# Rotary embedding on one core: the first load grows from 512 rows to 1024, and one table layout serves all tiles

## The chip, the core and the metric

The kernel runs on one core of a Trainium2 chip. The metric is device time in microseconds (us), the median over runs. Five engines work side by side: TensorE (PE), VectorE (DVE), ScalarE (ACT), GpSimd (POOL) and SyncE (SP). Each executes its own instructions in order and waits on semaphores for the others. Transfers (DMAs) are issued from the instruction streams of ACT and SP here, and 16 DMA engines, which both queues share, carry them out.

## The reference

`x` is 16 batches x 512 sequence positions x 1024 values in float32 (33.6 MB); `cos` and `sin` have 512 rows of 32 values. Each row of 1024 values is 16 heads of 64, and each head is rotated:

```python
x = x.reshape(batch, seq, num_heads, head_dim)
x1, x2 = x[..., :half_dim], x[..., half_dim:]
cos = cos[None, :, None, :]; sin = sin[None, :, None, :]
rotated = concatenate([x1 * cos - x2 * sin, x1 * sin + x2 * cos], axis=-1)
```

So for every row: t1 = x times cos, t2 = (x with the halves of each head swapped) times (-sin, +sin), and the result is t1 + t2. The table row depends on the sequence position alone.

## The kernel before

**Units.** The work is cut into 64 units `u` (the code's `rows`): a unit is 128 partitions x 1024 values, so 128 rows of `x`. Eight units, 0 to 7, 8 to 15 and so on, are called a group here: 1024 rows of `x`, 4 MB. A group is 8 slots of the ring `x_sb`, which holds 5 groups; results are written over the inputs in the ring and stored from there.

**Tiles.** A tile is what one DMA loads and one DMA stores. Batches 0, 1, 14 and 15 are `singles`: 512 rows, 4 per partition, 2 MB. The twelve batches between are taken in pairs, 8 rows per partition, 4 MB. So the first and the last group consist of two tiles of four units each, and the other six groups of one tile each. In a pair tile, partition `2 s + b` holds rows `8 s` to `8 s + 7` of batch `b` of the pair.

**Tables.** A single needs cos and sin with four sequence positions per partition (partition `p`: 4p to 4p+3); a pair needs eight (partitions 2s and 2s+1: 8s to 8s+7). The tables are loaded once into `stage` in the layout of singles. For singles, DVE copies cos to PSUM (L273) and ACT writes (-sin, +sin) to `s1_sb` (L183, L184). For pairs, two TensorE matmuls with a 0/1 matrix `pick`, made from the identity matrix, gather the rows into `pair_ps` (L209); ACT then writes `s2_sb` (L187, L188), and DVE makes a small PSUM table for its own sine products just before the first pair (L280, L281).

**A unit.** DVE multiplies x by cos into one of three PSUM buffers (`mul`, L302). POOL multiplies the swapped x by the sine table into one of eight SBUF buffers `t2_sb` (L263), two units in one instruction where `G2` says so. In row 3 of each pair tile DVE does that product instead of POOL (`V2`, L295). The sum is made by DVE (`comb`, L313), or, for units 1, 3 and 5 of a group (`PE2`; in the first and last group only some of them), by TensorE, which adds t2 onto t1 in PSUM (L225), and ACT, which copies the sum back to the ring (L192).

**Order.** All orders are written out by hand. DVE runs `mul(u)` one unit ahead of `comb`. The loads of the first five groups are issued by ACT at the start: the first tile, the two tables, then the rest. The later loads stand in ACT's stream behind the copy of a unit: the load of group 5 behind unit 17, of group 6 behind unit 25, and the two of group 7 behind unit 33. Each first waits until the stores of the ring slots that it overwrites have landed (`sem_out[k]`, line 195; groups 0, 1 and 2). While ACT waits there, the copies behind it wait too, and DVE stops when it needs the PSUM buffer of a unit that ACT has not copied. SP issues the stores, each when its tile's last sums are done (line 160).

Of the kernel before, what the change touches and what calls it, by code (L numbers as in the profile page):

```python
# [6 lines left out]
def bass_split_heads_rope_kernel(  # L7
# [16 lines left out]
    batch, seq, dim = x.shape  # L24
# [12 lines left out]
    COPY = mybir.ActivationFunctionType.Copy  # L37


    singles = (0, 1, batch - 2, batch - 1)  # L40
    tiles = [(b, R1 if b in singles else R2) for b in range(batch) if b in singles or b % 2 == 0]
    NT = len(tiles)
    RING = 5 * R2

    rows = [(t, r) for t, (_, n) in enumerate(tiles) for r in range(n)]
    NU = len(rows)
    EARLY = (NU - RING) // R2


    V_ROW = 3  # L50
    PE2 = [R1 <= u < NU - R1 and u % R2 in (1, 3, 5) for u in range(NU)]
    V2 = [tiles[t][1] == R2 and r == V_ROW for t, r in rows]

    def count(flags):
        return [sum(flags[: u + 1]) for u in range(NU)]
# [16 lines left out]
    with ExitStack() as stack:  # L72
        x_sb = stack.enter_context(nc.sbuf_tensor([P, RING, H, 2, HALF], fp32))
        t2_sb = stack.enter_context(nc.sbuf_tensor([P, NT2, H, 2, HALF], fp32))
        stage = stack.enter_context(nc.sbuf_tensor([P, 2, R1 * HALF], fp32))
        s1_sb = stack.enter_context(nc.sbuf_tensor([P, R1, 2, HALF], fp32))
        s2_sb = stack.enter_context(nc.sbuf_tensor([P, R2, 2, HALF], fp32))
        ident = stack.enter_context(nc.sbuf_tensor([P, P], fp32))
        pick = stack.enter_context(nc.sbuf_tensor([P, 2, P // 2, 2], fp32))
        zero = stack.enter_context(nc.sbuf_tensor([P, BANK], bf16))  # L80
        tab_ps = stack.enter_context(nc.psum_tensor([P, BANK], fp32))
        pair_ps = stack.enter_context(nc.psum_tensor([P, 2, 2, R1, HALF], fp32))
        t1_ps = stack.enter_context(nc.psum_tensor([P, NT1, H * HD], fp32))
        sem_in = [stack.enter_context(nc.semaphore(f"in{t}")) for t in range(NT)]
        sem_out = [stack.enter_context(nc.semaphore(f"out{k}")) for k in range(EARLY)]
# [13 lines left out]
        sem_t = stack.enter_context(nc.semaphore("pairs"))  # L99
        sem_a = stack.enter_context(nc.semaphore("act"))  # L100

        c1_ps = tab_ps[:, 0:R1 * HALF].rearrange("p (r d) -> p r d", d=HALF)
        v_ps = tab_ps[:, R1 * HALF:R1 * HALF + HD].rearrange("p (t d) -> p t d", d=HALF)

        def c_of(t, r):
            return c1_ps[:, r, :] if tiles[t][1] == R1 else pair_ps[:, r // R1, 0, r % R1, :]

        x1 = x.rearrange("b (s r) d -> b s (r d)", r=R1)
        o1 = out.rearrange("b (s r) h d -> b s (r h d)", r=R1)
        x2 = x.rearrange("b (s r) d -> s b (r d)", r=R2)  # L110
        o2 = out.rearrange("b (s r) h d -> s b (r h d)", r=R2)
        xs = x_sb[:].rearrange("p n h t d -> p n (h t d)")

        def in_dram(single, pairs, t):
            b, n = tiles[t]
            return single[b] if n == R1 else pairs[:, b:b + 2, :]

        def in_sbuf(t):
            b, n = tiles[t]
            k = b * R1 % RING  # L120
            return x_sb[:, k:k + n].rearrange("p n h t d -> p (n h t d)")

        def where(u):
# [3 lines left out]
        def swapped(k):  # L127
            return x_sb[:, k, :, ::-1, :]

        def over_heads(table):  # L130
            return table[:, None, :, :].broadcast_to([P, H, 2, HALF])
# [16 lines left out]

        def stores_of(k):

            return sum(b * R1 // R2 == k for b, _ in tiles)

        def load(eng, t):
            eng.dma_start(in_sbuf(t), in_dram(x1, x2, t)).then_inc(sem_in[t], 16)  # L154

        def on_sync(sp):
            for u in range(NU):
                t, r, k = where(u)
                if r == tiles[t][1] - 1:
                    wait_added(sp, u)  # L160
                    k = u // R2
                    sp.dma_start(in_dram(o1, o2, t), in_sbuf(t)).then_inc(sem_out[k] if k < EARLY else sem_rest, 16)
            sp.wait_ge(sem_rest, 16 * sum(stores_of(k) for k in range(EARLY, NU // R2)))

        def on_scalar(ae):
            later = {}
            for t, (b, n) in enumerate(tiles):
                if b * R1 + n <= RING:
                    load(ae, t)
                else:  # L170

                    later.setdefault((b * R1 - RING) // R2 * R2 + R2 - 1 + LAG, []).append(t)
                if t == 0:
                    for i, (table, sem) in enumerate(((cos, sem_cos), (sin, sem_sin))):
                        ae.dma_start(stage[:, i, :], table.rearrange("(s r) d -> s (r d)", r=R1)).then_inc(sem, 16)  # L175

            ae.wait_ge(sem_i, 2)
            ae.activation(  # L178
                pick[:], ident[:].rearrange("q (s k) -> q k s", k=2)[:, :, :, None].broadcast_to([P, 2, P // 2, 2]), COPY
            ).then_inc(sem_g, 1)  # L180
            ae.wait_ge(sem_sin, 16)
            sv = stage[:, 1, :].rearrange("s (r d) -> s r d", d=HALF)
            ae.activation(s1_sb[:, :, 0, :], sv, COPY, scale=-1.0)  # L183
            ae.activation(s1_sb[:, :, 1, :], sv, COPY).then_inc(sem_s, 1)  # L184
            ae.wait_ge(sem_t, 2)
            s2 = s2_sb[:].rearrange("p (k r) t d -> p k r t d", r=R1)
            ae.activation(s2[:, :, :, 0, :], pair_ps[:, :, 1, :, :], COPY, scale=-1.0)  # L187
            ae.activation(s2[:, :, :, 1, :], pair_ps[:, :, 1, :, :], COPY).then_inc(sem_s, 1)  # L188
            for u in range(NU):
                if PE2[u]:  # L190
                    ae.wait_ge(sem_e, n_pe[u])
                    ae.activation(xs[:, u % RING, :], t1_ps[:, u % NT1, :], COPY).then_inc(sem_a, 1)  # L192
                for t in later.get(u, ()):
                    k = (tiles[t][0] * R1 - RING) // R2
                    ae.wait_ge(sem_out[k], 16 * stores_of(k))
                    load(ae, t)

        def on_tensor(pe):
# [4 lines left out]
                        t1_ps[:, k, b * BANK:(b + 1) * BANK], zero[:, 0:P], zero[:], start=True, stop=True  # L203
                    ).then_inc(sem_w, 1)
            pe.wait_ge(sem_g, 1)
            pe.wait_ge(sem_cos, 16)
            pe.wait_ge(sem_sin, 16)
            for k in range(2):
                pe.matmul(  # L209
                    pair_ps[:, k].rearrange("p c r d -> p (c r d)"),  # L210
                    pick[:, k].rearrange("q s b -> q (s b)"),
                    stage[:].rearrange("q c f -> q (c f)"),
                    start=True,
                    stop=True,
                ).then_inc(sem_t, 1)
# [19 lines left out]
        def on_gpsimd(pl):  # L235
# [11 lines left out]
            for u in range(NU):  # L247
                if V2[u] or (G2[u] and u % 2 == 1):
                    continue
                t, r, k = where(u)  # L250
                n = 2 if G2[u] else 1
                if (t, r) == (0, 0):
                    pl.wait_ge(sem_s, 1)
                if (t, r) == (2, 0):
                    pl.wait_ge(sem_s, 2)
                if r == 0:
                    pl.wait_ge(sem_in[t], 16)
                if n == 2 and u + 1 >= NT2:
                    pl.wait_ge(sem_m, u + 2 - NT2 + NT1)  # L259
                elif n == 1:  # L260
                    wait_t2_free(pl, u)
                table = (s1_sb if tiles[t][1] == R1 else s2_sb)[:, r:r + n]
                pl.tensor_tensor(  # L263
                    t2_sb[:, u % NT2:u % NT2 + n],
                    x_sb[:, k:k + n, :, ::-1, :],
                    table[:, :, None, :, :].broadcast_to([P, n, H, 2, HALF]),
                    mult,
                ).then_inc(sem_p, 1)

        def on_vector(ve):  # L270
            ve.memset(zero[:], 0.0).then_inc(sem_z, 1)  # L271
            ve.wait_ge(sem_cos, 16)
            ve.tensor_copy(c1_ps, stage[:, 0, :].rearrange("s (r d) -> s r d", d=HALF)).then_inc(sem_c, 1)  # L273
            ve.wait_ge(sem_c, 1)
            ve.wait_ge(sem_w, NT1 * EH)

            def pair_tables():
                ve.wait_ge(sem_s, 2)
                row = pair_ps[:, V_ROW // R1, 1, V_ROW % R1, :]
                ve.tensor_scalar_mul(v_ps[:, 0, :], row, -1.0).then_inc(sem_c, 1)  # L280
                ve.tensor_copy(v_ps[:, 1, :], row).then_inc(sem_c, 1)  # L281

            first_v = V2.index(True)

            def mul(u):
                t, r, k = where(u)
                if r == 0:
                    ve.wait_ge(sem_in[t], 16)
                if (t, r) == (2, 0):
                    pair_tables()  # L290
                if u == first_v:
                    ve.wait_ge(sem_c, 3)
                if V2[u]:
                    wait_t2_free(ve, u)
                    ve.tensor_tensor(t2_sb[:, u % NT2, :, :, :], swapped(k), over_heads(v_ps), mult)  # L295
                if u >= NT1:
                    v = u - NT1
                    if PE2[v]:
# [3 lines left out]
                ve.tensor_tensor(  # L302
                    t1_ps[:, u % NT1, :].rearrange("p (h d) -> p h d", d=HALF),
                    x_sb[:, k, :, :, :].rearrange("p h t d -> p (h t) d"),
                    c_of(t, r)[:, None, :].broadcast_to([P, 2 * H, HALF]),
                    mult,
                ).then_inc(sem_m, 1)

# [55 lines left out]
```

## Time and profile before

| what | value |
|---|---|
| time, median of 3 runs (lowest, highest) | 161.18 us (161.13, 161.49) |
| span of the profiled execution, first to last instruction | 159.6 us |
| median time less that span | 1.6 us |
| DMA moved, mean rate over the span | 67.25 MB, 421 GB/s |
| POOL busy, DVE busy | 131.7 us (82%), 129.6 us (81%) |
| PE busy, ACT busy | 64.4 us (40%), 24.3 us (15%) |

The execution that was profiled has no time of its own beside its span. The span runs from the first to the last instruction, and the last is SP's wait for the last store, so the span holds all transfers. Busy shares are averages over stages; which engine ends a stage has to be read from the stage.

### The profile page before, as it was taken

What the parts mean: (1) busy time and instruction counts of PE and PEld (TensorE: products, weight loads), DVE (VectorE), ACT (ScalarE), POOL (GpSimd) and SP (SyncE); (2) the same over time, 40 slices, a digit from 0 to 9 for tenths busy, and PEclk for the clock granted to TensorE, in tenths of its full rate; (3) what the DMA queues carried; (4) which work ended last, traced back from release to release, by engine and by line L of the source; (5) the groups of instructions that cost most, each with busy time, mean ns of one, the idle gap of its engine ahead of it and who ended that gap; (6) DMA issues with size and microseconds to landing.
All of it is one profiled execution on the core that took longest, in us unless ns stands there. A gap on an engine that the chain in (4) does not pass through costs nothing.

```text
span 159.6 us, 499 instructions
## 1 busy us (share of the span) xinstructions
PE 64.4 (40%) x94; PEld 22.2 (14%) x94; DVE 129.6 (81%) x117; ACT 24.3 (15%) x27; POOL 131.7 (82%) x41
## 2 busy tenths in 40 slices
PE   6050017076408870789067400575058506900000
PEld 1020011021102220222021100211021102300000
DVE  0069947999999989998999629999999999556900
ACT  0420002004300250023102040023202310220000
POOL 1069999999999999999999798992999999089400
PEclk9999999759985589557759985589957995585555
DMA  5999999999999999999999999999999999999997
GB/s 144 396 466 472 394 411 431 448 476 402 394 448 406 495 419 402 476 435 402 443 435 435 394 476 435 402 460 394 427 456 448 443 394 423 472 419 435 386 456 300
DMA packets 3169, 67.25 MB, mean 421 GB/s; under 512 B 352, under 2 KB 608, under 8 KB 608
## 3 DMA queue, kind: packets, MB, share of 16 engines
q10 hardware_dynamic: 1728, 33.69, 49.8%
q1 hardware_dynamic: 1440, 33.56, 48.9%
q14 instruction: 1, 0.01, 0.0%
HBM read 33.69 MB, written 33.55 MB: 421 GB/s over the span
## 4 chain that ended last, share of the span: by engine, by line
DMA 61%; DVE 17%; POOL 5%; PE 5%; issue 4%; ACTq 1%; ACT 1%; DVEq 0%; POOLq 0%; SPq 0%
DMA x_sb<-in_x_dram 43%; DMA out_dram<-x_sb 18%; DVE t_ps L302 8%; DVE x_sb L313 7%; POOL t_sb L263 5%; PE t_ps L225 5%; DVE t_sb L295 2%; ACT x_sb L192 1%; ACTq L154 1%; ACTq L175 1%; DVE tab_ps L280 0%; DVEq L312 0%; DVE tab_ps L281 0%; DVEq L299 0%; POOLq L259 0%
## 5 line engine op out<-in xcount | busy, mean ns | idle before, releaser
L263 POOL TENSOR_TENSOR t_sb<-x_sb,s_sb 128x2048 f32<-128x2048 f32 (+1 forms) x35 | 131.0, 3784 | 17.1 <-DMA x_sb<-in_x_dram 8.3
L225 PE MATMUL t_ps<-t_sb,ident 128*128 128x512 f32 x84 | 59.6, 857 | 69.1 <-DVE t_ps L302 56.7
L302 DVE TENSOR_TENSOR t_ps<-x_sb,pair_ps 128x1024 f32<-128x1024 f32 x48 | 57.5, 1221 | 5.2 <-ACT x_sb L192 5.2
L313 DVE TENSOR_TENSOR x_sb<-t_ps,t_sb 128x1024 f32<-128x1024 f32 x43 | 52.2, 1216 | 5.9 <-POOL t_sb L263 5.9
L192 ACT ACTIVATE x_sb<-t_ps 128x1024 f32<-128x1024 f32 x21 | 21.4, 1024 | 107.6 <-PE t_ps L225 99.9
L225 PEld LDWEIGHTS t_ps<-t_sb,ident 128*128 128x128 f32 x84 | 20.3, 267 | 108.2 <-DVE t_ps L302 78.7
L302 DVE TENSOR_TENSOR t_ps<-x_sb,tab_ps 128x1024 f32<-128x1024 f32 x16 | 19.2, 1222 | 2.6 <-DMA x_sb<-in_x_dram 2.5
L295 DVE TENSOR_TENSOR t_sb<-x_sb,tab_ps 128x1024 f32<-128x1024 f32 x6 | 7.3, 1209 | 0.0
L273 DVE COPY tab_ps<-stage 128x128 f32<-128x128 f32 x1 | 0.3, 296 | 7.6 <-DMA stage<-in_cos_dram 7.6
L209 PE MATMUL pair_ps<-stage,pick 128*128 128x256 f32 x4 | 2.0, 667 | 5.1 <-DMA stage<-in_sin_dram 5.1
L202 PE MATMUL t_ps<-zero 128*128 128x512 bf16 x6 | 2.7, 629 | 1.3 <-DVE zero L271 1.3
L178 ACT ACT_TABLE_LOAD x1 | 1.3, 1283 | 5.5 <-issue 5.5
L209 PEld LDWEIGHTS pair_ps<-stage,pick 128*128 128x128 f32 x4 | 1.2, 324 | 6.1 <-issue 6.0
L202 PEld LDWEIGHTS t_ps<-zero 128*128 128x128 bf16 x6 | 0.7, 136 | 2.4 <-DVE zero L271 1.2
L271 DVE MEMSET zero<- 128x256 uint32 x1 | 0.3, 272 | 0.9 <-PEq L346 0.9
L187 ACT ACTIVATE s_sb<-pair_ps 128x256 f32<-128x256 f32 x1 | 0.4, 384 | 1.7 <-PE pair_ps L209 1.7
L183 ACT ACTIVATE s_sb<-stage 128x128 f32<-128x128 f32 x1 | 0.3, 310 | 1.8 <-DMA stage<-in_sin_dram 1.8
L236 POOL MEMSET ident<- 128x128 f32 x1 | 0.2, 205 | 0.3 <-POOLq L346 0.3
L178 ACT ACTIVATE pick<-ident 128x256 f32<-128x256 f32 x1 | 0.4, 416 | 0.0
L188 ACT ACTIVATE s_sb<-pair_ps 128x256 f32<-128x256 f32 x1 | 0.4, 377 | 0.0
L238 POOL TENSOR_SCALAR_AFFINE_SELECT ident<-ident 128x128 f32<-128x128 f32 x1 | 0.3, 295 | 0.1
L346 POOL MEMSET const-float32-0.0<- 128x1 f32 x1 | 0.1, 99 | 0.3 <-issue 0.3
(6 smaller groups left out, 1.0 us busy)
## 6 DMA issues: line engine op xcount, KB each, us to landing
x_sb<-in_x_dram ACTq DMA_DIRECT2D x6, 4096.0 KB, 38.7
out_dram<-x_sb SPq DMA_DIRECT2D x6, 4096.0 KB, 25.3
x_sb<-in_x_dram ACTq DMA_DIRECT2D x4, 2048.0 KB, 22.7
out_dram<-x_sb SPq DMA_DIRECT2D x4, 2048.0 KB, 16.1
stage<-in_cos_dram ACTq DMA_DIRECT2D x1, 64.0 KB, 7.5
stage<-in_sin_dram ACTq DMA_DIRECT2D x1, 64.0 KB, 7.2
```

Of the source, the lines that this page charges most:

```text
L154: eng.dma_start(in_sbuf(t), in_dram(x1, x2, t)).then_inc(sem_in[t], 16)
L175: ae.dma_start(stage[:, i, :], table.rearrange("(s r) d -> s (r d)", r=R1)).then_inc(sem, 16)
L178: ae.activation(pick[:], ident[:].rearrange("q (s k) -> q k s", k=2)[:, :, :, None].broadcast_to([P, 2, P // 2, 2]), COPY).then_inc(sem_g, 1)
L187: ae.activation(s2[:, :, :, 0, :], pair_ps[:, :, 1, :, :], COPY, scale=-1.0)
L192: ae.activation(xs[:, u % RING, :], t1_ps[:, u % NT1, :], COPY).then_inc(sem_a, 1)
L202: pe.matmul(t1_ps[:, k, b * BANK:(b + 1) * BANK], zero[:, 0:P], zero[:], start=True, stop=True).then_inc(sem_w, 1)
L209: pe.matmul(pair_ps[:, k].rearrange("p c r d -> p (c r d)"), pick[:, k].rearrange("q s b -> q (s b)"), stage[:].rearrange("q c f -> q (c f)"),
L225: ins = pe.matmul(t1_ps[:, u % NT1, b * BANK:(b + 1) * BANK], ident[:], t2[:, b * BANK:(b + 1) * BANK], start=False, stop=True, skip_group ...
L263: pl.tensor_tensor(t2_sb[:, u % NT2:u % NT2 + n], x_sb[:, k:k + n, :, ::-1, :], table[:, :, None, :, :].broadcast_to([P, n, H, 2, HALF]), ...
L295: ve.tensor_tensor(t2_sb[:, u % NT2, :, :, :], swapped(k), over_heads(v_ps), mult)
L302: ve.tensor_tensor(t1_ps[:, u % NT1, :].rearrange("p (h d) -> p h d", d=HALF), x_sb[:, k, :, :, :].rearrange("p h t d -> p (h t) d"), c_of ...
L313: ve.tensor_tensor(xs[:, k, :], t1_ps[:, u % NT1, :], t2_sb[:, u % NT2, :, :, :].rearrange("p h t d -> p (h t d)"), add,).then_inc(sem_v, 1)
```

## The change

All groups but the last become one tile of 1024 rows, the first group too. The rows of a tile are now numbered straight through: partition `64 b + s` holds rows `8 s` to `8 s + 7` of batch `b` of the pair, so a tile is 4 MB in one piece in DRAM, and no longer two batches interleaved partition by partition. The last group has the same layout but is loaded and stored in two halves, rows 0 to 3 and rows 4 to 7 of each partition (2 MB each, 16 KB pieces).

With one layout for all tiles there is one set of tables. `cos` and `sin` are loaded into 64 partitions, eight positions each. One matmul for each table, with `pick` now the 64 x 64 identity twice side by side, spreads it over 128 partitions, cos to `cos_bank` and sin to `sin_bank`. ACT makes one table `s_sb` from `sin_bank`. DVE's copy of cos (L273) and ACT's two copies for singles (L183, L184) are gone. DVE reads cos from `cos_bank` for all units; for its own sine products it uses two rows of `sin_bank` next to each other, the lower of which it overwrites with the negated row 3 (`v_table`, one small instruction, in the first group).

Since the first group is one tile, its unit 3 is now among the `V2` units: DVE makes that product, and POOL has one unit fewer (57 instead of 58). The issue points of the loads in ACT's stream, the sizes of the ring and of the buffers, and the split of the sums between DVE and TensorE stay.

```diff
-    singles = (0, 1, batch - 2, batch - 1)
-    tiles = [(b, R1 if b in singles else R2) for b in range(batch) if b in singles or b % 2 == 0]
+    runs = batch // 2
+    tiles = []
+    for c in range(runs):
+        if c == runs - 1:
+            tiles += [(c, 0, R1), (c, R1, R1)]
+        else:
+            tiles.append((c, 0, R2))
...
-        x2 = x.rearrange("b (s r) d -> s b (r d)", r=R2)
-        o2 = out.rearrange("b (s r) h d -> s b (r h d)", r=R2)
+        xr = x.rearrange("(c b) (s r) d -> c (b s) r d", b=2, r=R2)
+        outr = out.rearrange("(c b) (s r) h d -> c (b s) r (h d)", b=2, r=R2)
...
-                        ae.dma_start(stage[:, i, :], table.rearrange("(s r) d -> s (r d)", r=R1)).then_inc(sem, 16)
+                        ae.dma_start(stage[:, i, :], table.rearrange("(s r) d -> s (r d)", r=R2)).then_inc(sem, 16)
...
-            ae.wait_ge(sem_sin, 16)
-            sv = stage[:, 1, :].rearrange("s (r d) -> s r d", d=HALF)
-            ae.activation(s1_sb[:, :, 0, :], sv, COPY, scale=-1.0)
-            ae.activation(s1_sb[:, :, 1, :], sv, COPY).then_inc(sem_s, 1)
             ae.wait_ge(sem_t, 2)
-            s2 = s2_sb[:].rearrange("p (k r) t d -> p k r t d", r=R1)
-            ae.activation(s2[:, :, :, 0, :], pair_ps[:, :, 1, :, :], COPY, scale=-1.0)
-            ae.activation(s2[:, :, :, 1, :], pair_ps[:, :, 1, :, :], COPY).then_inc(sem_s, 1)
+            ae.activation(s_sb[:, :, 0, :], sin_ps, COPY, scale=-1.0)
+            ae.activation(s_sb[:, :, 1, :], sin_ps, COPY).then_inc(sem_s, 1)
...
-            pe.wait_ge(sem_cos, 16)
-            pe.wait_ge(sem_sin, 16)
-            for k in range(2):
+            for i, (table_ps, sem) in enumerate(((cos_ps, sem_cos), (sin_ps, sem_sin))):
+                pe.wait_ge(sem, 16)
                 pe.matmul(
...
-            ve.wait_ge(sem_cos, 16)
-            ve.tensor_copy(c1_ps, stage[:, 0, :].rearrange("s (r d) -> s r d", d=HALF)).then_inc(sem_c, 1)
-            ve.wait_ge(sem_c, 1)
             ve.wait_ge(sem_w, NT1 * EH)
+            ve.wait_ge(sem_t, 1)
+
+            def v_table():
+                ve.wait_ge(sem_s, 1)
+                ve.tensor_scalar_mul(sin_ps[:, V_ROW - 1, :], sin_ps[:, V_ROW, :], -1.0).then_inc(sem_c, 1)
...
-                if (t, r) == (2, 0):
-                    pair_tables()
+                if u == first_v - 1:
+                    v_table()
```

## The prediction

> **What bounds the kernel now.** I read the stretches of the span first, then the DMA queues, then the waits, then the timeline at the places where compute stops.
>
> Busy time by stretch (start:end, length, busy us of each engine with counts, granted PE clock, DMA share, GB/s):
> ```profile
> 0.00:1.80 1.80, 0.55 (x2) 0.28 (x3) 0.27 (x1) 0.00 (x0) 0.70 (x6) 1.00 0.00 0
> 1.80:3.40 1.60, 1.60 (x6) 0.46 (x4) 0.00 (x0) 0.00 (x0) 0.00 (x0) 1.00 1.15 225
> 3.40:20.00 16.60, 2.64 (x6) 1.18 (x4) 10.65 (x10) 2.87 (x6) 10.45 (x5) 1.00 1.01 428
> 60.00:100.00 40.00, 17.26 (x24) 5.91 (x24) 35.17 (x32) 6.04 (x6) 38.21 (x11) 0.72 1.00 433
> 100.00:140.00 40.00, 21.80 (x32) 7.43 (x32) 37.75 (x34) 7.34 (x8) 33.18 (x8) 0.77 1.01 433
> 140.00:158.40 18.40, 0.00 (x0) 0.00 (x0) 9.24 (x8) 0.86 (x1) 9.12 (x3) 0.56 0.98 421
> 158.40:159.60 1.20, 0.00 (x0) 0.00 (x0) 0.00 (x0) 0.00 (x0) 0.00 (x0) 0.50 0.23 96
> ```
> The last two figures say it: from 1.8 us to 158.4 us the 16 DMA engines are never idle, at 433 GB/s once started. No compute engine is full everywhere. Compute matters only if it leaves the DMA engines without a queued transfer, or issues the last store late.
>
> DMA engine time of a packet, from the DMA queue lines of two windows in which one size moves alone (packets, MB, share of 16 engines; 155 to 158 us, then 15 to 20 us):
> ```profile
> q1 hardware_dynamic: 78, 1.28, 99.3%
> q10 hardware_dynamic: 64, 2.10, 97.0%
> ```
> 78 packets of 16 KB in 99.3% of 16 x 3 us: 0.611 us each. 64 packets of 32 KB in 97.0% of 16 x 5 us: 1.2125 us each. So one 32 KB packet is 0.0095 us cheaper than two of 16 KB. A 4 MB tile of 128 packets of 32 KB is 8 per engine: 9.7 us alone, 19.4 us when the other queue takes every second packet.
>
> Waits:
> ```profile
> POOL t_sb L263 <- DMA x_sb<-in_x_dram: 8.3, 3, 4.3
> POOL t_sb L263 <- ACT s_sb L184: 8.2, 1, 8.2
> DVE t_ps L302 <- ACT x_sb L192: 5.2, 3, 4.4
> ```
> POOL waits for loads three times, so it has spare time in the middle. Its 8.2 us are the start. DVE's 4.4 us are seen in the timeline:
> ```profile
> 92.04 1.53 ACTq L154 DMA_DIRECT2D x_sb<-in_x_dram  x2
> 93.61 1.94 ACT L192 ACTIVATE x_sb<-t_ps 128x1024 f32<-128x1024 f32 x2 [7.78 <-issue]
> 94.67 2.36 DVE L302 TENSOR_TENSOR t_ps<-x_sb,pair_ps 128x1024 f32<-128x1024 f32 x2 [4.41 <-ACT x_sb L192]
> ```
> ACT stands before the loads of group 7 until group 2's store has landed (92.0), and DVE behind it. Last, the store that ends the run:
> ```profile
> 151.88 0.34 SPq L162 DMA_DIRECT2D out_dram<-x_sb  x1
> ```
> From the first load (issued 0.81, first packet at 1.8) a transfer needs 1.0 us to its first packet, so this one can move from 152.9. Packets end at 159.2 (0.4 us of landing before the span's end), and its 8 x 0.611 = 4.9 us begin at 154.3: even the last store waited 1.4 us for the DMA engines.
>
> **What the change does to the DMA sum.** Before: 1024 packets of 16 KB (four singles, in and out) and 1536 of 32 KB. After: 512 and 1792. That is 256 times 0.0095 us over 16 engines: -0.15 us. The tables go from 256 packets of 512 B to 128 of 1 KB; the line through the two sizes leaves 0.0095 us for a packet beside its bytes: -0.08 us. Two transfers fewer have 32 completion packets less; if these cost the same, -0.02 us. Together -0.24 us, off the path itself while the engines stay full.
>
> **What it does to the start.** The tables now queue behind 4 MB, not 2 MB: 2 MB more is 8 x 0.611 = 4.9 us. Cos landed at 8.7, now 13.6. Then DVE's copy (0.3 us) and ACT's two copies (0.6 us) for singles are gone, but both wait for TensorE. One matmul is two records of 634 ns; from 9.07 the first ended at 10.3 (1.2 us) and ACT started behind the second after 2.1 us. So DVE's first product starts at 13.6 + 0.05 + 1.2 = 14.85 (before 9.11), and POOL's, behind two ACT copies of 0.28 and 0.38 us, at 16.45 (before 9.55). The 64-partition matmul has no row; I give it the 128-partition one's time, half as lower and double as upper bound (up to 2 us more).
>
> POOL needs 2.31 us for one unit and 4.48 us for two (start to start). Its first group was four single units and two pairs, 18.2 us, to 27.7; now three and two, 15.9 us, to 32.35: +4.6. DVE idles at first until POOL's unit 0 (18.85), then has 13 instructions of 1.135 us and the small table before the product of unit 8, with some 0.2 us of waits for POOL: 33.9 against 29.2: +4.7. The first store is issued at 36.2, all 4 MB in one; before, 2 MB went at 20.2 and 2 MB at 31.6. None of this idles a DMA engine: four more tiles, 38.8 us of loads, are queued behind the first.
>
> **The ledger of the DMA engines after** (packets alternate between the queues when both have work):
> - Group 0 and the tables: to 13.2; group 1 to 22.9, group 2 to 32.6. At 37.2 store 0 joins, with half of group 3 done.
> - Shared: store 0 to 56.6, store 1 to 76, store 2 to 95.4. Loads: group 3 at 47.2, group 4 at 66.6, group 5 at 86, group 6 at 105.4. SP issues store 1 at 52 and store 2 at 68.4 (before 47.46 and 63.81, plus 4.6): in time. ACT issues loads 5 and 6 at 57.5 and 76.5, 9 us before the queue runs out.
> - Store 2 lands at 96.0 (before 92.0), so ACT and DVE resume 4.0 us later: DVE at 98.7. From there DVE ran without a wait to 137.7; I shift that by 4.0 to 4.1.
> - The halves of group 7 are 16 KB packets against the stores' 32 KB, so 4.9 + 9.7 = 14.6 us each: 120 and 134.6, landing at 135 (before 140.3). DVE wants the last half at 141.8: its wait of 2.5 us and POOL's of 4.3 us vanish. POOL's load waits at 91.9 and 111.2 go too; it meets DVE's unit 40 at 103.4 and is done with unit 61 at 141.6 and unit 63 at 146.2.
> - DVE's last eight instructions: 141.8 + 9.1 = 150.9. Last store issued at 151.0, movable from 152.0.
> - Stores alone from 134.6: store 5 to 139.2, store 6 to 148.9 (issued 136.3), the first half of group 7 to 153.8 (issued 145), the second to 158.7 plus the engines' unevenness, 0.4 us.
>
> So every store is queued before its turn, the tightest by about 2 us (store 6: movable 137.3, turn 139.2; the last: 152.0 and 153.8). DVE's added product (1.2 us) and POOL's missing one lie inside the shift of group 0. The start delay of 5 to 7 us is hidden by queued loads early, and by the earlier last load at the end. The span ends at 159.6 - 0.24 = 159.4, and with the 1.6 us outside it the median goes from 161.18 to 160.94.
>
> **Two rules of the Trainium skill.** Perfetto Trace Analysis, DMA Optimizations, speaks against the change: splitting DMAs lets work start sooner, where the DMA engines are generally idle. By it, joining the first loads would cost the 4.9 us of the start. Here the engines' share is 1.00 to 1.01, so its condition is not met; the trace cannot show the joined load yet. DMA: Bandwidth & Descriptors, Anatomy of one DMA, speaks for it: about 2 us are fixed for each DMA (stated for another issue path), so two fewer could save up to 4 us, an estimate. The trace bears that out for the first and last transfer alone (1.8 us before the first packet, 0.4 us after the last); in between no stretch shows a gap.
>
> **Rivals.**
> (a) Compute is late, slower. Store 0's issue sets store 2's landing (three shared stores, 58.2 us later), that sets when ACT and DVE resume, and that sets the last store. This chain passes any delay on one for one, and it decides once it is about 1.8 us later than I worked out. For it: the 64-partition matmul may cost up to 2 us more than I gave it; the granted PE clock of 0.72 to 0.77 may make ACT's copies later. Against: DVE's pace between stops is read over five groups. A chain 3 us late gives 160.94 + 1.2 = 162.1; 4 us late, 163.1.
> (b) The start is exposed in full, as the first rule has it without its condition: DVE ends 5.7 us later than before instead of earlier. 151.9 + 5.7 = 157.6, then 1.0 + 4.9 + 0.4: span 163.9, time 165.5. It needs compute to have had no waits to give up; it has 6.6 us (4.1 + 2.5) on DVE.
> (c) Transfers have a fixed cost on the path, as in the second rule: two fewer would win a few tenths up to 2 x 1.8 = 3.6 us, 157.3 to 160.7. The packed stretches speak against it.
> (d) The new order of rows in DRAM changes a 32 KB packet's time. Each 1% is 1792 x 0.012 / 16 = 1.36 us, either way. The two layouts of before differ by 0.8% per byte (1.2125 against 2 x 0.611 us for 32 KB), which is all I have seen an order of rows change.
> That the change is not in effect is no rival: the changed instruction streams have nine loads and nine stores of these shapes.
>
> **Numbers.** The forecast, engines full throughout: 78%. (a) 13%, (b) 2%, (c) 4%, (d) 3%. About 0.2% (0.32 us) is what a measurement can tell from no change. The forecast, 160.94, lies 0.08 us short of the bound for faster (160.86), and the runs shown spread over 0.36 us; the ramp of the first packets (1.6 us at 225 GB/s) with 32 KB pieces and the engines' unevenness at the end can move it by 0.3 us. So I split its 78% into 37% faster, 38% same, 3% slower. With (c) and half of (d), 42% faster; with (a), (b) and half of (d), 20% slower. The range is the forecast's own, 160.6 to 161.3, reaching a little into (c) below and to a chain 2.5 us late above: 160.5 to 161.7.
>
> **What would show it.** Right: DMA share 1.0 from 1.8 to 158 us; q1 with 1296 packets (before 1440); first product at 14.9 (DVE) and 16.5 (POOL); first store issued near 36.2; ACT's loads of group 7 issued near 96; no DVE or POOL wait for the last load; last store issued near 151. Wrong: a stretch after 135 us with share under 0.97, a last store issued after 153, or 32 KB packets of other than 1.21 us.

## The result, and the profile after

The changed kernel takes 162.52 us (median of 6 runs, 161.85 to 163.42), the kernel before 161.31 us beside it (161.13 to 161.70). The ratio is 1.0073, with a 95% interval of 1.0049 to 1.0098: slower by 0.7%, 1.2 us. The forecast was 160.94 us, and the range ended at 161.7. Of the executions of the kernels below one, with the tables on the other queue, fell in a slower state of the chip (164.72 us); its ratio leaves it out, its median does not.

The profiled execution spans 160.9 us, with 1.4 us outside it. The same stretches as before the change (busy us of each engine, granted PE clock, DMA share, GB/s):

```profile
3.40:20.00 16.60, 2.64 (x6) 1.16 (x4) 3.19 (x3) 2.25 (x4) 3.27 (x2) 1.00 1.00 418
60.00:100.00 40.00, 18.34 (x31) 5.85 (x29) 35.19 (x32) 6.03 (x6) 40.00 (x10) 0.83 1.00 432
100.00:140.00 40.00, 17.26 (x24) 5.78 (x24) 38.33 (x34) 8.08 (x8) 36.31 (x11) 0.74 0.98 420
140.00:158.40 18.40, 6.65 (x8) 2.37 (x8) 13.99 (x13) 2.05 (x2) 9.03 (x3) 0.59 0.97 413
158.40:160.90 2.50, 0.00 (x0) 0.00 (x0) 0.00 (x0) 0.00 (x0) 0.00 (x0) 0.50 0.74 315
```

From 3.4 to 20 us 418 GB/s move instead of 428; to this the experiments come back. From 20 to 100 us the DMA engines are as full as before. Then they are not: 420 GB/s instead of 433 from 100 to 140 us. Compute now works into the last stretch (14.0 us of DVE from 140 to 158.4, before 9.2). The packet records of the trace show the two places. Before the store of group 6 (near 140.2 us) 14 of the 16 engines stand idle, 0.4 to 1.1 us each, and before the last store (near 155.4 us) 15 of them, 0.2 to 0.8 us. Before the change no engine had such a gap. The transfers that move are the ones forecast; from the page of the changed kernel (packets, MB, share of 16 engines):

```profile
q10 hardware_dynamic: 1456, 33.69, 49.5%
q1 hardware_dynamic: 1296, 33.56, 48.5%
```

The engines with a long wait, from the list of waits (us in total, times, longest):

```profile
POOL t_sb L254 <- ACT s_sb L182: 15.4, 1, 15.4
DVE t_ps L289 <- PE cos_bank L202: 14.0, 1, 14.0
ACT x_sb L186 <- DMA out_dram<-x_sb: 10.1, 2, 7.2
DVE t_ps L289 <- ACT x_sb L186: 7.8, 6, 4.0
```

The first two are the late start. The waits for loads are gone, as forecast. The third has grown (7.8 us before, put down to "issue"): ACT stands before the later loads until stores have landed, and DVE behind it. The same place as in the timeline before, now at 99 us:

```profile
99.29 0.87 ACTq L155 DMA_DIRECT2D x_sb<-in_x_dram  x2
100.21 1.94 ACT L186 ACTIVATE x_sb<-t_ps 128x1024 f32<-128x1024 f32 x2 [7.20 <-DMA out_dram<-x_sb]
101.26 2.36 DVE L289 TENSOR_TENSOR t_ps<-x_sb,cos_bank 128x1024 f32<-128x1024 f32 x2 [4.02 <-ACT x_sb L186]
```

The loads of group 7 are issued at 99.29 (92.04 before, 96 forecast), and DVE goes on at 101.26 (94.67 before, 98.7 forecast). The last store:

```profile
154.54 0.33 SPq L163 DMA_DIRECT2D out_dram<-x_sb  x1
```

It is issued 3.5 us later than forecast and ends the span 6.3 us later: the 1.0 + 4.9 + 0.4 us of a transfer that finds its engines idle.

### The profile page after: what moved, and what is told of

Read it like the earlier page. It is cut to its first block, busy times and chain, and to the rows that moved or that the text cites. A ratio compares the mean times of both kernels' runs of the same rounds, so it can differ in the third digit from the quotient of the medians.

```text
span 160.9 us, 491 instructions
## 1 busy us (share of the span) xinstructions
PE 65.2 (41%) x94; PEld 22.2 (14%) x94; DVE 130.1 (81%) x116; ACT 23.5 (15%) x25; POOL 129.3 (80%) x40
## 3 DMA queue, kind: packets, MB, share of 16 engines
q1 hardware_dynamic: 1296, 33.56, 48.5%
## 4 chain that ended last, share of the span: by engine, by line
POOL 65%; issue 10%; DMA 8%; DVE 7%; PE 4%; ACT 1%; ACTq 0%; DVEq 0%
POOL t_sb L254 65%; DMA stage<-in_cos_dram 8%; DVE x_sb L300 4%; DVE t_ps L289 3%; PE t_ps L218 2%; PE cos_bank L202 1%; ACT x_sb L186 1%; PE sin_bank L202 1%; ACT s_sb L181 0%; ACTq L155 0%; ACT s_sb L182 0%; DVEq L299 0%; DVEq L286 0%
## 5 line engine op out<-in xcount | busy, mean ns | idle before, releaser
L254 POOL TENSOR_TENSOR t_sb<-x_sb,s_sb 128x2048 f32<-128x2048 f32 (+1 forms) x34 | 128.6, 3818 | 19.1 <-ACT s_sb L182 15.4
L289 DVE TENSOR_TENSOR t_ps<-x_sb,cos_bank 128x1024 f32<-128x1024 f32 x64 | 76.7, 1222 | 21.8 <-PE cos_bank L202 14.0
L218 PE MATMUL t_ps<-t_sb,ident 128*128 128x512 f32 x84 | 60.4, 867 | 70.6 <-DVE t_ps L289 70.6
L282 DVE TENSOR_TENSOR t_sb<-x_sb,sin_bank 128x1024 f32<-128x1024 f32 x7 | 8.5, 1214 | 0.0
L202 PE MATMUL cos_bank<-stage,pick 64*128 64x256 f32 x2 | 1.2, 696 | 9.9 <-DMA stage<-in_cos_dram 9.9
L202 PEld LDWEIGHTS cos_bank<-stage,pick 64*128 64x128 f32 x2 | 0.5, 306 | 10.8 <-issue 10.8
L181 ACT ACTIVATE s_sb<-sin_bank 128x256 f32<-128x256 f32 x1 | 0.4, 383 | 9.8 <-PE sin_bank L202 9.8
L202 PE MATMUL sin_bank<-stage,pick 64*128 64x256 f32 x2 | 1.1, 631 | 0.0
L202 PEld LDWEIGHTS sin_bank<-stage,pick 64*128 64x128 f32 x2 | 0.7, 333 | 0.2
L182 ACT ACTIVATE s_sb<-sin_bank 128x256 f32<-128x256 f32 x1 | 0.4, 378 | 0.0
```

Of the source, the lines that this page charges most:

```text
L181: ae.activation(s_sb[:, :, 0, :], sin_ps, COPY, scale=-1.0)
L182: ae.activation(s_sb[:, :, 1, :], sin_ps, COPY).then_inc(sem_s, 1)
L202: pe.matmul(table_ps.rearrange("p r d -> p (r d)"), pick[:].rearrange("q b s -> q (b s)"), stage[:, i, :], start=True, stop=True,).then_in ...
L218: ins = pe.matmul(t1_ps[:, u % NT1, b * BANK:(b + 1) * BANK], ident[:], t2[:, b * BANK:(b + 1) * BANK], start=False, stop=True, skip_group ...
L254: pl.tensor_tensor(t2_sb[:, u % NT2:u % NT2 + n], x_sb[:, k:k + n, :, ::-1, :], table[:, :, None, :, :].broadcast_to([P, n, H, 2, HALF]), ...
L289: ve.tensor_tensor(t1_ps[:, u % NT1, :].rearrange("p (h d) -> p h d", d=HALF), x_sb[:, k, :, :, :].rearrange("p h t d -> p (h t) d"), cos_ ...
```

## Experiments: the late start

**One theory** (S): the tables behind 4 MB make compute start late, group 0's only store goes out late, the stores land late, ACT and DVE resume late, and the last stores are late. **Its first rival** (R): the new row order in DRAM, or the tables through TensorE, costs the time. Ratios below are to the kernel before, run beside each.

**The first group in halves again.** Row order and tables stay as changed. Unit 3 of the first group, no longer in a tile of eight rows, goes back from DVE to POOL.

```diff
-            if c == runs - 1:
+            if c in (0, runs - 1):
```

> Changed kernel with the first group, too, loaded and stored in two halves of 2 MB; row order, tables and all else as changed. Theory S (the late start: tables behind 4 MB, first store late, group 2's store lands late, ACT and DVE resume late, last store late): DVE's first product near 10.1 us (15.2 in the changed kernel, 9.1 before), the last store is issued by 153, and the time is that of the kernel before or 0.1 to 0.2 us less: 161.0 to 161.4. Rival R (the new order of rows in DRAM, or the tables through TensorE, costs the time): stays at 162.2 to 162.8.

161.94 us, ratio 1.0032 (1.0020 to 1.0044). DVE's first product is at 10.3 us, and no engine has a gap before the last stores. The last store in the timeline of SP:

```profile
150.42 0.33 SPq L163 DMA_DIRECT2D out_dram<-x_sb  x1
```

It is issued 4.1 us earlier, so the links of S hold, and about half of the 1.2 us is back. The other half is not, which S had not expected. The stretches of the same kernel show where the run now ends:

```profile
159.50:160.00 0.50, 0.00 (x0) 0.00 (x0) 0.00 (x0) 0.00 (x0) 0.00 (x0) 0.50 0.08 33
```

A DMA share of 0.08 is about one engine of sixteen. The other fifteen have ended by 159.2, as before the change; one works on to 160.2.

**The later loads two units later.** The start stays late; only ACT's wait moves.

```diff
-    LAG = 10
+    LAG = 12
```

> Changed kernel with LAG 12 instead of 10: the later loads stand two units further back in ACT's stream, so ACT has copied two more units before it waits for the stores of groups 0, 1 and 2. Start as late as in the changed kernel (first store issued near 37). Theory S with the wait in ACT as its link: DVE's wait of 4.0 us near 97 shrinks to under 1 us, last store issued near 150 to 151, time 160.9 to 161.3. Rival: if the late start acts without that wait (POOL or DVE simply end late), 162.2 to 162.8; if the later loads starve the DMA engines, slower than 162.8.

161.88 us, ratio 1.0040 (1.0026 to 1.0054). DVE's wait in the timeline falls from 4.02 to 1.27 us:

```profile
100.30 1.23 DVE L289 TENSOR_TENSOR t_ps<-x_sb,cos_bank 128x1024 f32<-128x1024 f32 x1 [1.27 <-ACT x_sb L186]
```

The last store, in the timeline of SP, goes out 4.9 us earlier:

```profile
149.68 0.33 SPq L163 DMA_DIRECT2D out_dram<-x_sb  x1
```

The stretch from 154.6 to 155.6 us in the changed kernel:

```profile
154.60:155.60 1.00, 0.00 (x0) 0.00 (x0) 0.00 (x0) 0.00 (x0) 0.00 (x0) 0.50 0.66 279
```

And here (the share counts packets by their start, so it can pass 1):

```profile
154.60:155.60 1.00, 0.00 (x0) 0.00 (x0) 0.00 (x0) 0.00 (x0) 0.00 (x0) 0.50 1.07 459
```

The gap is gone, without touching the start: ACT's wait is the link through which the late start reached the end. But again only 0.6 us come back. Thirteen engines end at 158.5 to 159.1, three at 160.1. In the changed kernel all sixteen end between 160.3 and 160.5. I read this so: there, engines that had fallen behind used the idle time to catch up, and without the idle time they end last.

**The same two kernels once more**, for what repeats.

> The changed kernel once more. If the late stores are what idles the engines at the end, all engines have gaps of 0.4 to 1 us before the store of group 6 (near 140 us) and before the last store (near 155 us) again, and the last store is issued after 153. Time 162.0 to 162.8.

162.33 us, ratio 1.0069 (1.0050 to 1.0088). The gaps are there again, 0.7 to 1.5 us on 14 engines near 140.5 and 0.5 to 0.8 us on 15 near 155.8, and the last store is issued at 154.93. They belong to the kernel.

> The changed kernel with LAG 12 once more, tables over 64 partitions. If the slow packets behind the tables belong to the 64 partitions, all 16 engines have them again near 12.7 us, 0.3 to 0.5 us; three engines ended 1.2 us behind the others: if that is scatter, their number and lag differ now. Time 161.6 to 162.2.

161.91 us, ratio 1.0034 (1.0020 to 1.0048). No gaps. The packets behind the tables are slow again on all 16 engines, by 0.2 us (1.45 against 1.21). This time no engine ends more than 0.5 us behind the mean (159.4 against 158.9). The execution that was profiled took 161.25 us, one of the three shortest of eight (161.2 to 161.4, the others 161.9 to 162.1); the earlier one, with three engines 1.1 us behind the mean, took 161.90. So how far engines lag at the end scatters from one execution to the next, and so does the time.

**A late start in the kernel before.**

```diff
-                if t == 0:
+                if t == 1:
                     for i, (table, sem) in enumerate(((cos, sem_cos), (sin, sem_sin))):
```

> Kernel before (old row order, old tables, first group in two halves) with the table loads issued behind the second 2 MB tile, so that compute starts about 4.9 us later, near 14 us. Theory S: group 0's second store lands near 58 us instead of 53, group 2's near 97 (before 92), last store issued near 153 or later; the time rises from 161.3 to between 161.6 and 162.6. Rival R: stays at 161.3.

161.55 us, ratio 1.0016 (1.0004 to 1.0029). Group 0's second store landed at 59.3 and group 2's at 98.2, the last store went out at 153.22, and some engines had gaps of 0.1 to 0.2 us near 139.5. The direction is S's; the price is 0.3 us, just under the range expected. There is slack of about 1.3 us in the last store of the kernel before, and this delay used it up. The 0.3 us itself is no proof of S: counted from the packet records, about as much is lost on slow load packets between 28 and 34 us, and the gaps come to under 0.1 us over the sixteen engines.

**A still later start.** The changed kernel with the same edit, which puts the tables behind the second 4 MB tile.

> Changed kernel (LAG 10) with the tables behind the second 4 MB tile: compute starts 9.7 us later, near 24.9 us. Theory S (a late start passes one for one through the store of group 2, ACT's wait and DVE to the last store): last store issued near 164, DMA engines idle for about 10 us before the end, time 171 to 172.5. Rival H (queued loads hide a late start, as the prediction had it for 5 to 7 us): under 166.

166.79 us, ratio 1.0340 (1.0322 to 1.0358): between the two expectations. A start 9.9 us later (25.1 against 15.2) moved the last store by 4.5 us. The waits tell why:

```profile
DVE t_ps L289 <- ACT x_sb L186: 2.4, 6, 0.5
```

DVE waited 5.4 us less for ACT than in the changed kernel. By the time that store 0 was ready, few of the first loads were left; it had the engines to itself for most of its time and landed at 62.8 (61.5 in the changed kernel). So a late start is not passed on one for one; what DVE waits anyway is taken off. Nor do queued loads hide it any longer. When store 0 is done they have run out, and all 16 engines stand idle for 1.3 to 2.2 us until store 1 moves at 63.6:

```profile
62.00:64.00 2.00, 0.12 (x1) 0.12 (x1) 2.00 (x3) 0.00 (x0) 2.00 (x2) 0.50 0.61 262
```

**The tables ahead of the tile.** The loop of the two table loads moves ahead of the first `load`.

> Changed kernel with the two table loads issued ahead of the first tile's load, 4 MB tile as changed. Theory S: tables are there by 4 us, DVE and POOL start when the tile lands, near 13.9 us (15.2 and 16.7 in the changed kernel); group 0 is done 2 to 3 us earlier, first store issued near 34.3 (37.0), last store near 152, time 161.0 to 161.6. Rival R: 162.2 to 162.8, since row order and tables through TensorE are the same.

162.99 us, ratio 1.0108 (1.0090 to 1.0127), slower still. The start did come earlier (DVE and POOL at 14.6), the last store was issued at 153.24, and the gaps before it vanished. The price is at the other end. The first stretch in the changed kernel:

```profile
0.00:3.20 3.20, 1.95 (x5) 0.72 (x6) 0.27 (x1) 0.00 (x0) 0.70 (x6) 1.00 0.61 164
```

And with the tables first:

```profile
0.00:3.20 3.20, 1.95 (x5) 0.73 (x6) 0.27 (x1) 0.00 (x0) 0.70 (x6) 1.00 0.14 41
```

With small transfers first, the large packets begin 1.5 us later (3.3 against 1.8), and engines that are never idle afterwards cannot make that up. Another half microsecond on every engine goes near 38 us, where the first store joins; this loss comes back below.

## Experiments: what is left without the gaps

In the trace's packet records a second loss shows: behind the tables, the next large packet of each engine is slow. I took this apart with the gaps removed (LAG 12).

**The tables on the other queue.**

```diff
         def on_sync(sp):
+            for i, (table, sem) in enumerate(((cos, sem_cos), (sin, sem_sin))):
+                sp.dma_start(stage[:, i, :], table.rearrange("(s r) d -> s (r d)", r=R2)).then_inc(sem, 16)
```

> LAG 12 as in the run with loads two units later (161.88 there), and the two table loads are issued by SP at the start, on the queue of the stores, instead of by ACT behind the first tile. Theory Q (a large packet that follows the 1 KB table packets on its own queue is slow: 1.69 instead of 1.21 us on all 16 engines at 12.7 us in that run): tables land by 5 us, compute starts at 13.7, the slow packets at 12.7 are gone, nothing new replaces them, time 161.2 to 161.6. Rival Q2: the table packets cost their half microsecond wherever they go (1.5 us were lost at the start with the tables ahead of the tile on one queue): 161.8 to 163.

162.98 us, ratio 1.0104 (1.0063 to 1.0145). The expectation failed at its first step: cos landed at 12.7 us and sin at 18.0.

```profile
20.09 42.91 POOL L253 TENSOR_TENSOR t_sb<-x_sb,s_sb 128x1024 f32<-128x1024 f32 x12 [18.72 <-ACT s_sb L181]
```

POOL starts at 20.1. SP issued cos at 0.80, but its first packet moved at 6.1. From there the queues alternate packet by packet: an engine's 1 KB packets come 1.3 us apart, each behind a 32 KB packet of the other queue. The run says little on the slow packets.

**The old row order**, 4 MB first tile and tables as changed.

```diff
-        xr = x.rearrange("(c b) (s r) d -> c (b s) r d", b=2, r=R2)
-        outr = out.rearrange("(c b) (s r) h d -> c (b s) r (h d)", b=2, r=R2)
+        xr = x.rearrange("(c b) (s r) d -> c s b r d", b=2, r=R2)
+        outr = out.rearrange("(c b) (s r) h d -> c s b r (h d)", b=2, r=R2)
```

> LAG 12, tables behind the first tile as changed, but the rows of a tile go back to the order of the kernel before (partition 2s+b, two batches interleaved) in all loads, stores and tables. Theory R (the new row order in DRAM costs DMA time, by slow packets or by engines that lag at the end): 161.2 to 161.5, engines end within 0.8 us of each other. Rival: row order is neutral and the rest of the loss comes from the 4 MB start and the table packets: 161.7 to 162.0, as with the new order.

162.50 us, ratio 1.0070 (1.0053 to 1.0088): slower, not faster, than with the new order (161.88), and four engines ended over 0.7 us behind the mean. The slow packets behind the tables are there too (1.56). The new row order is not where the time went.

**Smaller table packets.**

```diff
-                        ae.dma_start(stage[:, i, :], table.rearrange("(s r) d -> s (r d)", r=R2)).then_inc(sem, 16)
+                        for h in range(2):
+                            ae.dma_start(
+                                stage[:, i, h * R1 * HALF:(h + 1) * R1 * HALF],
+                                table.rearrange("(s h r) d -> h s (r d)", h=2, r=R1)[h],
+                            ).then_inc(sem, 16)
```

> LAG 12, new row order, but each table is loaded by two DMAs of 64 partitions x 512 B instead of one of 64 x 1 KB: 256 packets of 512 B as in the kernel before. Theory Q1 (the size of the table packets makes the next large packet slow): the packets at 12.7 us take 1.21 again, time 161.4 to 161.7. Rival: the slow packets stay (they come from the large packets being 32 KB, or from 64 partitions): 161.8 to 162.0.

162.01 us, ratio 1.0040 (1.0027 to 1.0054), and the packets behind the tables took 1.63 us on all 16 engines. The size of the table packets is not it.

**The tables over 128 partitions again**, spread by four matmuls instead of two; the first tile stays 4 MB.

```diff
-                        ae.dma_start(stage[:, i, :], table.rearrange("(s r) d -> s (r d)", r=R2)).then_inc(sem, 16)
+                        ae.dma_start(stage[:, i, :], table.rearrange("(s r) d -> s (r d)", r=R1)).then_inc(sem, 16)
```

> LAG 12, new row order and 4 MB first tile, but the tables are loaded over 128 partitions (512 B each) as in the kernel before and spread by four matmuls. Theory P (a load into 64 partitions is what makes the next large packet slow on every engine, 0.3 to 0.5 us, whatever the size of its packets, and leaves engines lagging): the packets at 13 us take 1.21, no engine ends over 0.8 us behind the others, time 161.2 to 161.5. Rival P2 (the 4 MB first tile with its 32 KB packets does it): 161.8 to 162.1 with slow packets as before.

The slow packets are gone, yet the time is 162.23 us, ratio 1.0053 (1.0036 to 1.0071). In their place all engines lost 0.4 to 1.3 us near 39.5, where the first store joins the loads.

> The kernel with LAG 12, 4 MB first tile and tables over 128 partitions once more. It lost 0.5 to 0.6 us on every engine at 39 us, where the first store joins. If that loss belongs to this kernel, it is there again, time 162.0 to 162.5. If it is scatter between executions, it is smaller now, and the time is 161.4 to 161.9.

162.13 us, ratio 1.0056 (1.0038 to 1.0075), with the loss near 40 us on all engines again. But the loss is not this kernel's alone. In the second execution of LAG 12 with tables over 64 partitions, the 16 load packets ahead of the first store, from 39.5 to 40.0 us, are slow as well (packets, MB, share of 16 engines; 1.63 us each):

```profile
q10 hardware_dynamic: 16, 0.52, 326.6%
```

In the first execution of the same kernel they took 1.30 us. Over all 18 profiles the last 16 load packets ahead of the first store take 1.21 to 1.35 us on the mean in eleven, and 1.63 to 1.91 us in seven. All four profiles of changed kernels with tables over 128 partitions are among the seven, and three of the ten with tables over 64. What makes these packets slow is open. With a 4 MB first tile the tables over 128 partitions bring nothing.

**A 64-partition load by itself.** The kernel before, with two more table loads into spare memory, which nothing reads; once over 64 partitions, once over 128.

```diff
+                    for i, table in enumerate((cos, sin)):
+                        ae.dma_start(spare[:, i, :], table.rearrange("(s r) d -> s (r d)", r=R2)).then_inc(sem_x, 16)
```

> Kernel before with two more table loads of 64 partitions x 1 KB into spare memory, right behind its own; nothing reads them. The bytes and packets alone are 0.37 us of engine time. Theory P: slow large packets behind them (0.2 to 0.5 us on all engines), time 161.7 to 162.3. Rival P2: no slow packets, 161.4 to 161.6.

> The same with the two spare loads over 128 partitions x 512 B (0.43 us of engine time). Theory P: no slow packets, 161.5 to 161.7, less than the 64-partition one by 0.2 to 0.6. Rival P2: the same as the 64-partition one.

Over 64 partitions 162.57 us, ratio 1.0074 (1.0053 to 1.0096), above the range expected. Over 128 partitions 161.66 us, ratio 1.0027 (1.0017 to 1.0037). The same bytes, and the intervals lie apart. From 8 to 12 us, over 64 partitions:

```profile
8.00:12.00 4.00, 2.01 (x4) 1.17 (x4) 2.38 (x3) 1.01 (x4) 1.53 (x1) 1.00 1.10 370
```

Over 128 partitions:

```profile
8.00:12.00 4.00, 2.04 (x4) 1.17 (x4) 2.65 (x3) 1.50 (x5) 2.25 (x1) 0.50 1.08 440
```

The same share of busy time moves 370 instead of 440 GB/s. The mean time of the 16 large packets that follow the table loads, from the packet records of all runs in which the tables come behind a tile on the same queue:

```
tables over   large packet   its usual time   behind the tables
64 partitions     32 KB        1.21 us        1.45 to 1.78 us  (7 profiles)
64 partitions     16 KB        0.61 us        0.83, 1.17 us    (2 profiles)
128 partitions    32 KB        1.21 us        1.21 us          (3 profiles)
128 partitions    16 KB        0.61 us        0.61 us          (4 profiles)
```

Why a load into 64 partitions does this, no run shows.

**Halves and 128-partition tables**, then the same with LAG 12.

> LAG 10, new row order, first group in two halves, tables over 128 partitions: against the kernel before only the row order and the way of the tables through TensorE are left. Theory P: 161.1 to 161.4, no slow packets at 8 us. If the row order costs after all: 161.7 to 162.

> New row order, first group in two halves, tables over 128 partitions, and the later loads two units further back (LAG 12): all three suspected costs taken away at once. If they are all of it: 161.0 to 161.3, no idle engines before the end, no slow packets at 8 us. If the engines that lag or the loss where the first store joins belong to the new row order or its tables through TensorE: 161.5 to 162.

161.49 us, ratio 1.0016 (1.0004 to 1.0027), and 161.40 us, ratio 1.0015 (1.0002 to 1.0027). Both lie just above the range expected, but with the three suspected costs away, all but about 0.2 us of the 1.2 is back. The second kernel's last stretches:

```profile
100.00:140.00 40.00, 24.59 (x32) 8.47 (x32) 38.96 (x35) 8.19 (x8) 34.80 (x9) 0.67 1.00 433
158.40:160.00 1.60, 0.00 (x0) 0.00 (x0) 0.00 (x0) 0.00 (x0) 0.00 (x0) 0.50 0.12 51
```

433 GB/s as before the change; what is left is in the last line, an engine or two that end behind the others (mean end 158.9, last 159.6; before the change 158.9 and 159.2). The loss where the first store joins is there in both kernels. In the second, from 24.6 to 25.2 us, 1.65 us for each of 16 load packets:

```profile
q10 hardware_dynamic: 16, 0.52, 274.8%
```

No version beat the kernel before.

## Why the prediction was wrong, step by step

**The failed step** is in the ledger: that a store can move 1.0 us after its issue, and that "at 37.2 store 0 joins". The 1.0 us was read from the first load, which found idle engines. Store 0 was issued at 36.99 in the changed kernel. The DMA queues from there to 40.9 us:

```profile
q10 hardware_dynamic: 48, 1.57, 96.9%
```

Not one packet of q1: store 0 begins at 41.0, after 4.0 us. Each engine had about three 32 KB load packets ahead of it (48 packets, 16 engines). The trace of before had this row, and the forecast did not use it; its first store was issued at 20.19, and from 20.2 to 23.8:

```profile
q10 hardware_dynamic: 61, 1.47, 98.0%
```

There the first store's first packet moves at 23.9, and in all 18 profiles of this case it moves 3.5 to 4.9 us after the issue. On top, a store counts as landed when its slowest engine is done: fifteen had landed by 59.9, the last at 61.5. So store 0 landed at 61.5, where the ledger has the end of its packets at 56.6; store 2 landed at 99.3 instead of 96.0. Group 6's store was issued at 139.26, after its turn at 139.2 (forecast 136.3), and the last store at 154.54 instead of 151.0. These are the two places where the engines stand idle. Of the 3.8 us by which store 0 joined late, 0.8 are its later issue and 3.0 the step named. With 41.0 in place of 37.2 the ledger itself gives 99.8 for store 2, 154.8 for the last store and 162.7 us.

Rival (a), given 13%, has this price too: a chain 3.5 us late gives 160.94 + 3.5 - 1.8 = 162.6 by its terms, and 162.52 was measured. In both sums the agreement is in part luck. They say that without the late chain the time is 160.94, but with LAG 12, where no engine is idle before the last stores, it is 161.9. The ledger's 0.4 us for the engines' unevenness was too small there: the last engine ended 1.1 and 0.5 us behind the mean in two profiles. In the changed kernel it is 0.1 us, which I read as engines evening out in the idle time. Nor was the cause of the delay one that (a) named, and its "one for one" was wrong in general (9.9 us later moved the last store by 4.5).

**What DVE gave up.** Its first product came 6.1 us later (forecast 5.7), the waits inside fell from 13.6 us (5.2 for ACT, 5.9 for POOL, 2.5 for a load) to 9.4 (7.8 for ACT, 1.6 for POOL), and its busy time rose by 0.5: 6.1 - 4.2 + 0.5 = 2.4 us, against 2.7 us by which the last store was late. The forecast had seen that waits would be given up; it had not seen that the wait for ACT would grow by 2.6.

**The DMA sum** was -0.24 us. The packet counts came out as forecast, 1296 on q1, and 32 KB packets mostly took 1.21 us. The tables' term, -0.08, was wrong in sign: the 64-partition loads made the next packet slower on every engine, by 0.3 and 0.6 us on the mean in the changed kernel's two profiles, a cost for which the trace of before has no row. The range had no bound for it. Of the gain in the DMA sum nothing showed in the time.

**Right steps:** the start (14.85 and 16.45 forecast for DVE and POOL, 15.2 and 16.7 measured, of which 0.15 to 0.2 us is the later landing of cos), the first store's issue within 0.8 us (36.2; 36.99), no wait for the last load, and that the engines stay full while loads are queued. Rivals (b) and (c) did not occur. For (d), a cost of the new row order, the run that undoes it speaks against: with the old order the time went up.

**The two rules.** The Trainium skill, Perfetto Trace Analysis, DMA Optimizations, ties the gain of splitting to DMA engines that are generally idle. Here their share was 1.00, and splitting the first tile still won half of the loss back: what counts is whether they would be idle at the end. The fixed cost that the Trainium skill, DMA: Bandwidth & Descriptors, Anatomy of one DMA, gives for each DMA on another issue path did not show here: two transfers fewer saved nothing that the runs can tell.

**How the 1.2 us divide.** About 0.6 us is idle engines before the last stores: two edits in different places, the halves and LAG 12, each removed the gaps and brought that back. This half is shown. The other half is not lost by all engines alike. With the gaps gone the mean of the sixteen ends is 158.9 us (halves) and 159.0 (LAG 12), against 158.9 before the change, but the last engine ends 1.3 and 1.1 us behind that mean, against 0.4 before.

What makes engines lag is open. The tables over 64 partitions are a suspect and not proven for the changed kernel. As loads added to the kernel before they cost 0.9 us more than the same bytes over 128 partitions (162.57 against 161.66), which is clear. With the first group in halves the step to 128 partitions brought 0.45 us (161.94 to 161.49; the intervals overlap a little). With the 4 MB first tile the same step made the time longer (161.88 and 161.91, then 162.23 and 162.13). In both places the packets behind the tables became fast, and the load packets ahead of the first store were slow in every profile; with 64 partitions they were slow in one of three. Whether one brings the other is open too.

## What to carry to other kernels

Where the DMA engines are full, a late start is hidden only as long as the chain from the first store through the next ring slots to the last store is not late; work that chain out with the time that a transfer needs to join busy engines, read from a store in the middle of the trace and not from the first load. An instruction stream that issues loads should not stand before a store's landing while other engines need it: moving that wait two units back, the change of one number, returned half of the loss. Small loads are not free among large ones: two 64 KB tables one tile further back cost the kernel before 0.3 us and the changed kernel 4.3 us, and two more such loads cost the kernel before (161.22 beside them) 1.35 us over 64 partitions and 0.44 us over 128. And look at the end of every DMA engine, not at their mean share: the last one sets the time.

## What the runs showed of the hardware that I had not expected

- The first store, issued while loads kept the engines busy, moved its first packet after 3.7 us (kernel before) and 4.0 us (after), 3.5 to 4.9 us over all 18 profiles, against 1.0 us for the first load on idle engines. About three load packets per engine went first (40 to 50 in all).
- Loads into 64 partitions made the next large packet slower by 0.2 to 0.6 us on all 16 engines, in 9 of 9 profiles that have them behind a tile on the same queue; loads of the same bytes into 128 partitions did not, in 7 of 7.
- Two queues alternated packet by packet, 1 KB against 32 KB: 64 KB in 1 KB packets beside 32 KB packets landed at 12.7 us, the next 64 KB at 18.0.
- The last of the 16 engines ended 0.1 to 1.7 us behind their mean, 1.1 and 0.5 us in two profiles of one kernel, and the span ends with the last.
